# Gathered rows by each step's matmuls, a fixed order on ScalarE, and one later section of the top-k, in a hybrid S5 / mLSTM / PEER layer

## The chip, the cores and the metric

The kernel runs on one core of one Trainium2 chip. The metric is the device time of one execution in microseconds, from the first to the last instruction and what lies around them; lower is better. A core has TensorE (matrix products, "PE" in the profile, with "PEld" for its weight loads), VectorE ("DVE"), ScalarE ("ACT"), GpSimd ("POOL") and SyncE ("SP"), which here only starts transfers. Each engine works through its own queue in order, and waits on semaphores for the others.

## The reference

One decoder layer over 512 tokens of 1024 numbers, with 16 learned tokens ahead of them. A state-space branch and a matrix-memory branch are merged and added to the input; behind them comes a PEER layer, which holds 16384 experts of one neuron each. The change touches PEER alone:

```python
def block(xb):
    q = (xb @ w_q).astype(f32).reshape(PEER_TOKEN_BLOCK, PEER_HEADS, 2, PEER_HALF)
    s = jnp.einsum('thid,hikd->thik', q, keys32)
    sv, si = lax.top_k(s, PEER_TOPK)
    cand = sv[..., 0, :, None] + sv[..., 1, None, :]
...
    cs, ci = lax.top_k(cand, PEER_TOPK)
    eidx = jnp.take_along_axis(cidx, ci, axis=-1)
    gate = jax.nn.softmax(cs, axis=-1)
    ug = u_tab[eidx]
    act = jax.nn.gelu(jnp.einsum('td,thkd->thk', xb, ug).astype(f32))
    vg = v_tab[eidx]
    return jnp.einsum('thk,thkd->td', (gate * act).astype(vg.dtype), vg)
```

Each token has 8 heads; a head scores two sets of 128 keys and takes the best 16 of each, the best 16 of their sums name the experts (128 x 128 of them), and the token's output is the sum of the experts' rows of v, each weighted with its gate times the gelu of the token's product with the expert's row of u. The layer ends with a norm.

## The kernel before

The tokens are four tiles of 128. The kernel computes PEER in two ways side by side.

For 384 tokens (three tiles' worth, `SD`) it takes all experts as a dense product. The experts are 128 key columns of 128 experts each. For a column `j`, `hidden` (L1090) makes the products h of the column's block of u with 352 of those tokens (24 matmuls of 352 columns: eight blocks of the inner dimension, times three, since each operand is split into a high and a low part, and low times low is left out) and their gelu, `acts[j]`. The last 32 of the 384 are served through gathered rows in an earlier stage, whose values are copied. The gates of all 384 tokens, which are zero for most experts, come from DRAM tiles `gds` and `gd`. `w = gate * act` is then the weight matrix of the column, and `products` (L1593) adds w times the column's block of v to three PSUM accumulators (18 matmuls of 512 columns).

For one tile of 128 tokens it gathers rows instead: 128 rows per token from u and 128 from v, one row for all 128 tokens at a time (512 KB) by an indirect DMA on GpSimd (`fetch`, L1136). `use` (L1142) takes each: a product with the token and a sum for a row of u, a multiply-add into `ac0` for one of v. The first eight of these 256 are used ahead of the loop (`NEARLY`), 248 in it.

The loop over the columns (L1638 to L1699) is the last stage. In step `j`:
- `ready(j + 6)`: for 76 columns (`SP_`) the activations were made earlier and saved, and are loaded again in pairs; eight columns (`LEFT`) are made just ahead of the loop; for the other 44, which come in pairs, `hidden(j + 6)` splits the block of u (`uh` on ScalarE, `ul` on VectorE), makes h on TensorE and applies the gelu on ScalarE.
- the gates of eight columns at a time, `gin`, are loaded; the block of v is loaded (`raw`).
- VectorE multiplies `w`, ScalarE copies 32 columns more into it and makes its high part `wh` (L1656); `split` (L81) makes `vh` on ScalarE and `vl` on VectorE.
- gathered rows: `upto` says how many have to be used by the end of the step, an equal number a step. One is used ahead of `wl` (L1671, VectorE), the rest behind it.
- `products`, three times (the last three steps are done together by accumulator).

`wh`, `wl`, `vh` and `vl` have three buffers each, the PSUM tile of h two, the gathered rows seven.

What orders the instructions: a scheduler takes them in the order in which they are traced, moves each to where it expects it to be ready first, and so fixes each engine's queue before the run. `tc.keep_in_program_order(ins)` pins an instruction behind the one traced last on the same engine; `inorder` (L1061) does that inside the loop alone. In the loop VectorE's instructions are pinned; ScalarE's `vh`, copy, `wh`, `uh` and gelu are not.

Ahead of the loop, `scores(s)` (L1207) runs for 16 segments (8 heads times 2): a query product, its scores and their top 16 on VectorE. GpSimd makes the low part of each segment's weights (`wql`, in `split` with GpSimd). At segment 8 the generator `pairs_of(1, 0, 4)` (L1232) is run out: the candidates, their top 16, and the places of the chosen experts for four heads of token tile 1. It yields nine times; its last section (from L1298) makes the expert's number `ef`, the softmax, the offset `off` in the DRAM tile of gates, and turns both by 24 small matmuls into `xp`, from which GpSimd later scatters the gates column by column (`scatter`, from segment 13 on). `filled` puts pieces of `hidden` (a quarter column each) between the sections as work for TensorE.

Of the kernel before, what the change touches and what calls it, by code (L numbers as in the profile page):

```python
# [17 lines left out]
AF = mybir.ActivationFunctionType  # L18
# [5 lines left out]
P = 128  # L24
# [18 lines left out]
PH = 8  # L43
NKEY = 128
TOPK = 16
NSEG = 2 * PH
# [3 lines left out]
TB = 32  # L50
MS = TB
JB = 8
# [9 lines left out]
def f32(ap):  # L62
    return ap.bitcast(F32)
# [3 lines left out]
def tile_hybrid_block(ctx: ExitStack, tc: tile.TileContext, a: dict, out: bass.AP, dbg: dict | None = None):  # L67
    nc = tc.nc
    V, A, PE, GP, SY = nc.vector, nc.scalar, nc.tensor, nc.gpsimd, nc.sync
# [8 lines left out]
    ident = cst.tile([P, P], F32, name="ident")  # L78
    make_identity(nc, ident)

    def split(hi, lo, src, eng=V):  # L81
        A.activation(hi, src, AF.Copy)  # L82
        return eng.tensor_tensor(lo, src, f32(hi), op=OP.subtract)  # L83

    def mm3(ps, lh, ll, rh, rl, first, last, pin=None):
# [940 lines left out]
def peer(tc, a, out, dbg, cst, dram, xh, xl, blanks, ident, h2d, xsd, gds, x0, qt01, dump, split, mm3, rsqrt_cols):  # L1026
# [3 lines left out]
    V, A, PE, GP, SY = nc.vector, nc.scalar, nc.tensor, nc.gpsimd, nc.sync  # L1030
    NTD = NT - 1
    SD = NTD * P
    SDH = SD - MS
    RA = 6
    LEFT = 8
# [3 lines left out]
    SP_ = [2 * k + n for k in SPP for n in range(2)]  # L1039
    NEARLY = 8  # L1040
# [11 lines left out]
    with es:  # L1052
# [4 lines left out]
        ad = dram.tile([NSP, P, 2, SDH], F32, name="ad")  # L1057
        acts = {}
        loop = [False]

        def inorder(ins):  # L1061

            if loop[0]:
                tc.keep_in_program_order(ins)
            return ins
# [5 lines left out]
        def act_of(j):  # L1071

            k, n = divmod(j, 2)
            if k not in pairs_:
                pairs_[k] = up.tile([P, 2, SDH], F32, tag="act", name=f"act{k}", bufs=5)
            return (pairs_.pop(k) if n else pairs_[k])[:, n]

        def load(j, eng):

            k, n = divmod(j, 2)  # L1080
            if k not in uraw:
                uraw[k] = up.tile([P, 2, NK, P], F32, tag="uraw", name=f"u{k}", bufs=2)
                SY.dma_start(uraw[k], a["ut"][k])
            raw = (uraw.pop(k) if n else uraw[k])[:, n]
            hi = up.tile([P, NK, P], F32R, tag="uhi", name=f"uh{j}", bufs=3)
            lo = up.tile([P, NK, P], F32R, tag="ulo", name=f"ul{j}", bufs=3)
            inorder(split(hi, lo, raw, eng))
            return hi, lo

        def hidden(j, k0=0, k1=NK, eng=V, pin=False):  # L1090

            if k0 == 0:
                acts[j] = *load(j, eng), hps.tile([P, D // 2], F32, tag="h", name=f"h{j}")[:, :SDH]
            hi, lo, p = acts[j]
            clock[0] += (k1 - k0) * 0.48
            for k in range(k0, k1):
                mm3(p, hi[:, k], lo[:, k], xh[k // 4][:, k % 4, P:P + SDH], xl[k // 4][:, k % 4, P:P + SDH],
                    k == 0, k == NK - 1, tc.keep_in_program_order if pin and k == 0 else None)
            if k1 == NK:
                whole_ = pairs_.get(j // 2)  # L1100
                acts[j] = act_of(j)
                A.activation(acts[j], p, AF.Gelu_apprx_tanh)  # L1102
                if j in SP_:
                    acts.pop(j)
                    if j % 2:
                        SY.dma_start(ad[SPP.index(j // 2)], whole_)
# [430 lines left out]
        def filled(*of):  # L1537
            for us in pairs_of(*of):
                fill(us)
                yield  # L1540

        for s_ in range(NSEG):
            scores(s_)
            if s_ == 1:
                for r in range(P // MS):
                    SY.dma_start(xrep[MS * r:MS * (r + 1)], xsd)
            if s_ == NSEG // 2:
                for _ in filled(1, 0, PH // 2):
                    pass
            if s_ > NSEG - 4:  # L1550
                scatter(2)
# [25 lines left out]
        for j, h in todo:  # L1577
            hidden(j, 2 * h, 2 * h + 2)
# [56 lines left out]

        due = 0
        loop[0] = True
        for j in range(NKEY):  # L1638
            if j + RA < NKEY:
                ready(j + RA)  # L1640
            if j % JB == 0:
                gin = vp.tile([P, SD // TB, JB, TB], F32, tag="gin", name=f"gi{j}")
                i_ = SY.dma_start(gin[:, :HB], gds[:, j // JB])
                for o in heads[-1]:
# [3 lines left out]
            w = vp.tile([P, SD], F32, tag="w", name=f"w{j}", bufs=3)  # L1648
            raw = up.tile([P, D], F32, tag="vraw", name=f"v{j}", bufs=4)
            SY.dma_start(raw, a["v"][j // 2 * 2 * P:(j // 2 + 1) * 2 * P].rearrange("(p n) d -> p n d", n=2)[:, j % 2])  # L1650
            inorder(V.tensor_tensor(w[:, :SDH].rearrange("p (b t) -> p b t", t=TB), gin[:, :SDH // TB, j % JB],  # L1651
                                    acts.pop(j).rearrange("p (b t) -> p b t", t=TB), op=OP.mult))
            A.copy(w[:, SDH:], gin[:, SDH // TB, j % JB])
            wh = vp.tile([P, SD], F32R, tag="wh", name=f"wh{j}", bufs=3)
            wl = vp.tile([P, SD], F32R, tag="wl", name=f"wl{j}", bufs=3)
            A.activation(wh, w, AF.Copy)  # L1656
            vh = vp.tile([P, D], F32R, tag="vhi", name=f"vh{j}", bufs=3)
            vl = vp.tile([P, D], F32R, tag="vlo", name=f"vl{j}", bufs=3)
            inorder(split(vh, vl, raw))

            upto = min(j + 1, NKEY - 6) * (2 * P - NEARLY) // (NKEY - 6)
            for last in (0, 1):
                while due < (upto if last else min(due + 1, upto)):
                    n = NEARLY + due
# [115 lines left out]
```

## Time and profile before

| | |
|---|---|
| time, median of 3 runs | 1668.21 us (1667.74 to 1668.38) |
| profiled execution, its own time | 1670.1 us |
| its span | 1668.4 us |
| TensorE busy | 1620.0 us, 97% |
| VectorE busy | 1318.1 us, 79% |
| ScalarE busy | 708.3 us, 42% |
| GpSimd busy | 709.4 us, 43% |
| moved by DMA | 423.20 MB, mean 254 GB/s |
| the loop on TensorE, first to last product | 950.2 to 1656.6 us |

In a row of the timeline stand the start, the duration, engine, line, operation, the tiles written and read, shapes and a count; in square brackets, how long the engine was idle ahead of it and what ended that. A matmul's duration is modelled and overlaps the next one's, so the distance from start to start says what one costs. In a row of groups the mean is in nanoseconds. In a row of waits stand the engine and line that waited, what for, the total in us, how often, and the longest.

### The profile page before, as it was taken

How to read it: one execution, taken by the hardware profiler on the slowest of the kernel's cores; microseconds unless marked ns; L12 is line 12 of the kernel's file. 1: busy time of each engine (PE TensorE's matmuls, PEld its weight loads, DVE VectorE, ACT ScalarE, POOL GpSimd, SP SyncE). 2: the span in 40 equal slices, each digit the busy share in tenths (PEclk: the TensorE clock that was granted, in tenths of full speed). 3: DMA queues.
4: the chain of work that ended last, by engine and by line, in shares of the span. 5: the costliest groups of instructions: out<-in, count | busy, mean ns of one | idle time of the engine just before them, and what ended most of it. 6: DMA issues, size and time to landing. Idle time of an engine off the chain costs nothing.

```text
span 1668.4 us, 25647 instructions
## 1 busy us (share of the span) xinstructions
PE 1620.0 (97%) x9551; PEld 1429.4 (86%) x9551; DVE 1318.1 (79%) x2639; ACT 708.3 (42%) x1159; POOL 709.4 (43%) x474
## 2 busy tenths in 40 slices
PE   7999999999999999989999999999999999999997
PEld 7898787777889799989999888888888888888885
DVE  6996743366578899998798497988878989797976
ACT  4444554423333144565475533433343433343434
POOL 2000023213122477768877243434434756464630
PEclk9999999999999999999999999999999999999999
DMA  4514253113463256878999999999999999999973
GB/s 180 128 52 114 78 186 106 64 51 103 150 218 102 68 137 171 275 265 279 311 366 348 364 396 373 342 401 342 384 343 403 397 386 370 386 374 354 397 269 113
DMA packets 147957, 423.20 MB, mean 254 GB/s; under 512 B 38228, under 2 KB 56788, under 8 KB 138360
## 3 DMA queue, kind: packets, MB, share of 16 engines
q1 hardware_dynamic: 86184, 263.00, 43.9%
q0 software_dynamic: 55360, 151.07, 25.5%
q10 hardware_dynamic: 6288, 7.49, 1.4%
q8 instruction: 75, 1.23, 0.3%
q14 instruction: 50, 0.41, 0.1%
HBM read 376.13 MB, written 45.38 MB: 253 GB/s over the span
## 4 chain that ended last, share of the span: by engine, by line
PE 80%; DVE 8%; DMA 5%; ACT 2%; issue 2%; POOL 2%; ACTq 0%; DVEq 0%; POOLq 0%
PE o L86 10%; PE o L90 10%; PE o L89 10%; PE h L86 8%; PE h L90 8%; PE h L89 8%; PE q L89 1%; PE gp L1501 1%; PE q L90 1%; PE q L86 1%; DMA wo<-in_w_out 1%; PE s L877 1%; PE n L886 1%; POOL ge L1362 1%; DMA ge<-in_u,xsi 1%
## 5 line engine op out<-in xcount | busy, mean ns | idle before, releaser
L90 PE MATMUL h<-x2h,ul 128*128 128x352 f32 x1024 | 332.5, 325 | 5.3 <-DVE ul L83 5.3
L86 PE MATMUL h<-x2h,uh 128*128 128x352 f32 x1024 | 333.7, 326 | 3.7 <-ACT act L1102 1.8
L89 PE MATMUL h<-x2l,uh 128*128 128x352 f32 x1024 | 331.7, 324 | 0.0
L86 PE MATMUL o<-vh,wh 128*128 128x512 f32 x768 | 279.6, 391 | 7.7 <-ACT wh L1656 7.5
L89 PE MATMUL o<-vl,wh 128*128 128x512 f32 x768 | 278.9, 390 | 0.8 <-DVE vl L83 0.8
L90 PE MATMUL o<-vh,wl 128*128 128x512 f32 x768 | 266.3, 390 | 0.9 <-DVE wl L1671 0.9
L1139 POOL DMA_INDIRECT g<-in_v,e x128 | 202.2, 1580 | 146.5 <-DVE ac L1154 129.5
L82 ACT ACTIVATE uh<-u 128x1024 fp32r<-128x1024 f32 x128 | 135.2, 1059 | 224.5 <-PE h L89 170.9
L1139 POOL DMA_INDIRECT g<-in_u,e x120 | 135.2, 1126 | 214.1 <-DVE g L1146 195.4
L1421 POOL DMA_INDIRECT gds<-cw,ix x96 | 183.1, 1908 | 43.9 <-issue 28.6
L86 PEld LDWEIGHTS h<-x2h,uh 128*128 128x128 f32 x1024 | 193.4, 189 | 8.1 <-ACT act L1102 2.5
L90 PEld LDWEIGHTS h<-x2h,ul 128*128 128x128 f32 x1024 | 193.0, 189 | 8.0 <-DVE ul L83 6.7
L89 PEld LDWEIGHTS h<-x2l,uh 128*128 128x128 f32 x1024 | 193.2, 189 | 1.9
L82 ACT ACTIVATE vh<-v 128x1024 fp32r<-128x1024 f32 x128 | 135.1, 1057 | 132.9 <-PE o L90 116.0
L83 DVE TENSOR_TENSOR ul<-u,uh 128x1024 fp32r<-128x1024 f32 x128 | 155.4, 1217 | 26.6 <-ACT uh L82 26.5
L86 PEld LDWEIGHTS o<-vh,wh 128*128 128x128 f32 x768 | 143.4, 188 | 37.0 <-ACT wh L1656 9.9
L83 DVE TENSOR_TENSOR vl<-v,vh 128x1024 fp32r<-128x1024 f32 x128 | 155.8, 1217 | 22.7 <-ACT vh L82 22.6
L90 PEld LDWEIGHTS o<-vh,wl 128*128 128x128 f32 x768 | 144.1, 188 | 31.9 <-DVE wl L1671 1.6
L89 PEld LDWEIGHTS o<-vl,wh 128*128 128x128 f32 x768 | 144.2, 188 | 30.6 <-DVE vl L83 1.4
L1154 DVE SCALAR_TENSOR_TENSOR ac<-g,w,ac 128x1024 f32<-128x1024 f32 x127 | 162.2, 1277 | 0.1
L1146 DVE SCALAR_TENSOR_TENSOR g<-g,x 128x1024 f32<-128x1024 f32 x120 | 145.9, 1217 | 0.0
L1656 ACT ACTIVATE wh<-w 128x384 fp32r<-128x384 f32 x128 | 66.8, 522 | 143.5 <-DVE w L1651 141.5
(553 smaller groups left out, 3037.6 us busy)
## 6 DMA issues: line engine op xcount, KB each, us to landing
u<-in_ut SPq DMA_DIRECT2D x64, 1024.0 KB
v<-in_v SPq DMA_DIRECT2D x128, 512.0 KB
gd<-stg SPq DMA_DIRECT2D x9, 2048.0 KB
gi<-gd SPq DMA_DIRECT2D x16, 1152.0 KB
ad<-act SPq DMA_DIRECT2D x38, 352.0 KB
act<-ad SPq DMA_DIRECT2D x38, 352.0 KB
wq<-in_w_q SPq DMA_DIRECT2D x14, 512.0 KB
gds<-qt SPq DMA_DIRECT2D x6, 1024.0 KB
```

Of the source, the lines that this page charges most:

```text
L82: A.activation(hi, src, AF.Copy)
L83: return eng.tensor_tensor(lo, src, f32(hi), op=OP.subtract)
L86: i_ = PE.matmul(ps, lh, rh, start=first, stop=False)
L89: PE.matmul(ps, lh, rl, start=False, stop=False)
L90: return PE.matmul(ps, ll, rh, start=False, stop=last)
L877: PE.matmul(p[:, :w], xk[kk][:, c0:c0 + P], qt[:, kk, T - w:], start=kk == 0, stop=kk == 1)
L886: PE.matmul(p, pm[:, OFF[j] + (i - j) * P:OFF[j] + (i - j + 1) * P], vt[:, j], start=j == 0, stop=False)
L1139: return GP.indirect_dma_start(out=t, out_offset=None, in_=a["u"] if s_ < P else a["v"], in_offset=bass.IndirectOffsetOnAxis(ap=e0[:, c:c ...
L1146: i_ = V.scalar_tensor_tensor(g, g, 1.0, x0, op0=OP.mult, op1=OP.mult, accum_out=hsl[:, c:c + 1])
L1154: i_ = V.scalar_tensor_tensor(ac0, g, w0[:, c:c + 1], ac0, op0=OP.mult, op1=OP.add)
L1421: i_ = GP.indirect_dma_start(out=gds.rearrange("i g b j t -> (i g b j t)").unsqueeze(1), out_offset=bass.IndirectOffsetOnAxis(ap=ix[:, c:c ...
L1656: A.activation(wh, w, AF.Copy)
```

## The change

- The rows gathered in the loop are dealt out in proportion to the matmuls of each step. `steps` gives 18 x 0.227 for the products, and 24 x 0.161 more for a step in which h of a column is made; `upto` follows the running sum up to step 122.
- On ScalarE, `vh` of a step is pinned, then the 32-column copy, then `wh`, each behind the one before. The gelu of a column is no longer issued right behind its products h: the column is kept in `behind_v`, and the gelu follows `wh` of the next step, pinned. `uh` is as before. What VectorE does in a step keeps its order.
- Of the generator at segment 8 eight sections are run there, and the last one after the scores of segment 9.

```diff
-    def split(hi, lo, src, eng=V):
-        A.activation(hi, src, AF.Copy)
+    def split(hi, lo, src, eng=V, pin=lambda i_: i_):
+        pin(A.activation(hi, src, AF.Copy))
         return eng.tensor_tensor(lo, src, f32(hi), op=OP.subtract)
...
+        behind_v = []
...
             if k1 == NK:
+                if loop[0]:
+                    behind_v.append((j, p))
+                    return
                 whole_ = pairs_.get(j // 2)
                 acts[j] = act_of(j)
                 A.activation(acts[j], p, AF.Gelu_apprx_tanh)
...
             if s_ == NSEG // 2:
-                for _ in filled(1, 0, PH // 2):
+                first = filled(1, 0, PH // 2)
+                for _ in range(2 + PH // 2 + 2):
+                    next(first)
+            if s_ == NSEG // 2 + 1:
+                for _ in first:
                     pass
...
+        steps = [18 * 0.227 + (24 * 0.161 if LEFT <= j + RA < NKEY and j + RA not in SP_ else 0) for j in range(NKEY)]
         for j in range(NKEY):
...
-            A.copy(w[:, SDH:], gin[:, SDH // TB, j % JB])
             wh = vp.tile([P, SD], F32R, tag="wh", name=f"wh{j}", bufs=3)
             wl = vp.tile([P, SD], F32R, tag="wl", name=f"wl{j}", bufs=3)
-            A.activation(wh, w, AF.Copy)
             vh = vp.tile([P, D], F32R, tag="vhi", name=f"vh{j}", bufs=3)
             vl = vp.tile([P, D], F32R, tag="vlo", name=f"vl{j}", bufs=3)
-            inorder(split(vh, vl, raw))
-
-            upto = min(j + 1, NKEY - 6) * (2 * P - NEARLY) // (NKEY - 6)
+            inorder(split(vh, vl, raw, pin=tc.keep_in_program_order))
+            tc.keep_in_program_order(A.copy(w[:, SDH:], gin[:, SDH // TB, j % JB]))
+            tc.keep_in_program_order(A.activation(wh, w, AF.Copy))
+            while behind_v and behind_v[0][0] < j + RA:
+                n, p = behind_v.pop(0)
+                acts[n] = act_of(n)
+                tc.keep_in_program_order(A.activation(acts[n], p, AF.Gelu_apprx_tanh))
+
+            upto = min(int((2 * P - NEARLY) * sum(steps[:j + 1]) / sum(steps[:NKEY - 6]) + 1e-6), 2 * P - NEARLY)
             for last in (0, 1):
                 while due < (upto if last else min(due + 1, upto)):
```

## The prediction

> **What bounds the kernel now.** I read the page first (engine shares, the chain), then the waits of TensorE, then the loop's own rows.
>
> ```profile
> span 1668.4 us, 25647 instructions
> ...
> PE 1620.0 (97%) x9551; PEld 1429.4 (86%) x9551; DVE 1318.1 (79%) x2639; ACT 708.3 (42%) x1159; POOL 709.4 (43%) x474
> ...
> PE 80%; DVE 8%; DMA 5%; ACT 2%; issue 2%; POOL 2%; ACTq 0%; DVEq 0%; POOLq 0%
> ```
>
> TensorE is the bound: 97% busy and 80% of the chain. No part of the change takes a matmul away, so all it can win is TensorE's waiting. The next rows are TensorE's waits from 940 us to the end (the loop over the 128 key columns and what follows): engine and line that waited, what for, us in all, times, the longest. Behind them stands one window of that loop: engines' busy time, then granted clock, DMA's busy share and GB/s.
>
> ```profile
> PE o L86 <- ACT wh L1656: 7.5, 6, 1.7
> PE o L90 <- DVE wl L1671: 0.9, 1, 0.9
> PE o L89 <- DVE vl L83: 0.8, 1, 0.8
> PE h L86 <- ACT act L1102: 0.6, 1, 0.6
> ```
>
> ```profile
> 1300.00:1400.00 100.00, 100.00 (x489) 87.03 (x488) 90.12 (x100) 38.57 (x68) 62.65 (x38) 1.00 1.00 381
> ```
>
> In this window TensorE never stops (100.00 of 100 us). The loop has 9.8 us of visible waits in all, 7.5 of them for `wh`, the high part of w that ScalarE makes. What stands ahead of one such `wh` in ScalarE's queue (steps counted from the loop's first `vh` and `wh`):
>
> ```profile
> 1030.17 1.05 ACT L82 ACTIVATE vh<-v 128x1024 fp32r<-128x1024 f32 x1
> 1031.12 0.51 ACT L1656 ACTIVATE wh<-w 128x384 fp32r<-128x384 f32 x1
> 1033.16 1.06 ACT L82 ACTIVATE vh<-v 128x1024 fp32r<-128x1024 f32 x1 [1.53 <-PE o L90]
> ...
> 1041.15 1.06 ACT L82 ACTIVATE vh<-v 128x1024 fp32r<-128x1024 f32 x1 [3.67 <-PE o L90]
> 1042.12 0.20 ACT L1653 COPY w<-gi 128x32 f32<-128x32 f32 x1
> 1042.22 0.52 ACT L1656 ACTIVATE wh<-w 128x384 fp32r<-128x384 f32 x1
> ```
>
> ```profile
> 1033.28 0.52 DVE L1651 TENSOR_TENSOR w<-gi,act 128x352 f32<-128x352 f32 x1
> 1042.77 0.56 DVE L1671 TENSOR_TENSOR wl<-w,wh 128x384 fp32r<-128x384 f32 x1 [6.69 <-ACT wh L1656]
> ```
>
> ```profile
> 1040.91 0.32 PE L86 MATMUL h<-x2h,uh 128*128 128x352 f32 x1
> 1041.06 0.32 PE L89 MATMUL h<-x2l,uh 128*128 128x352 f32 x1
> 1042.80 0.73 PE L86 MATMUL o<-vh,wh 128*128 128x512 f32 x2 [1.41 <-ACT wh L1656]
> ...
> 1133.19 0.50 PE L86 MATMUL o<-vh,wh 128*128 128x512 f32 x1 [1.41 <-ACT wh L1656]
> 1223.48 0.50 PE L86 MATMUL o<-vh,wh 128*128 128x512 f32 x1 [1.36 <-ACT wh L1656]
> 1531.87 0.50 PE L86 MATMUL o<-vh,wh 128*128 128x512 f32 x1 [1.41 <-ACT wh L1656]
> 1621.93 0.50 PE L86 MATMUL o<-vh,wh 128*128 128x512 f32 x1 [1.73 <-ACT wh L1656]
> ```
>
> The three `vh` are those of steps 16, 17 and 18, the two `wh` those of 15 and 16. w of step 16 was ready at 1033.80 (1033.28 + 0.52), but its `wh` stands behind `vh` of step 18, which waits until the products of step 15 give its buffer back. So TensorE ends step 15, does two matmuls of h, and waits while ScalarE does `vh` 18, a copy and then `wh` 16. The cost of one is more than its idle time, since a matmul's end is modelled and overlaps the next: 1042.80 - 1041.06 is 1.74 us, where two such matmuls start 0.15 apart (1041.06 - 1040.91), so about 1.58 lost. The other three of 1.4 are alike; the last, idle 0.32 more, is 1.9. The five cost 4 x 1.58 + 1.9 = 8.2 us.
>
> **High part of v, then of w, then the last activation.** No instruction is added to the loop. `vh`, the 32-column copy, `wh` and the activation are pinned in this order on ScalarE, and the activation of a column whose products h were made in step j comes in step j + 1. For step 16 that is `vh` 16, copy, `wh` 16, and only then `vh` 17 and 18: `wh` 16 comes right behind w (1033.80) and is 6 us early for TensorE. The pin has a gap: in a step that also splits a u block (44 of 128), `vh` is pinned behind `uh`, which itself floats, so `vh` may stand ahead of an older `wh` there. Steps 16, 32, 48, 104 and 120, where the five waits lie, split none. I take all five as gone: -8.2 us (bounds 0 and -8.2). New waits: `wh` j now queues behind `vh` j, which waits for v's DMA and for the products of step j - 3; behind it are copy, `wh`, the activation, then VectorE's `wl`, then the products of j. But `wh` waits for the products of j - 3 anyway (three buffers each), and TensorE still has two steps to do. The later activation feeds w five steps on; two PSUM buffers hold h, and columns come in pairs with at least two steps between pairs. Both 0.
>
> **The loop's first step** pays for the pin, for the last instruction on ScalarE ahead of `vh` 0 is now the activation of column 7.
>
> ```profile
> 937.73 2.95 ACT L82 ACTIVATE vh<-v 128x1024 fp32r<-128x1024 f32 x3 [2.15 <-DMA gd<-stg]
> ...
> 951.01 0.80 ACT L1102 ACTIVATE act<-h 128x352 f32<-128x352 f32 x2
> ```
>
> ```profile
> 949.01 0.53 DVE L1651 TENSOR_TENSOR w<-gi,act 128x352 f32<-128x352 f32 x1 [6.13 <-DMA gi<-gd]
> 949.46 1.22 DVE L83 TENSOR_TENSOR vl<-v,vh 128x1024 fp32r<-128x1024 f32 x1
> 950.59 1.22 DVE L1146 SCALAR_TENSOR_TENSOR g<-g,x 128x1024 f32<-128x1024 f32 x1
> ...
> 951.74 0.56 DVE L1671 TENSOR_TENSOR wl<-w,wh 128x384 fp32r<-128x384 f32 x1
> ```
>
> ```profile
> 942.03 0.43 PE L86 MATMUL h<-x2h,uh 128*128 128x352 f32 x1 [0.56 <-ACT act L1102]
> ...
> 949.71 0.32 PE L90 MATMUL h<-x2h,ul 128*128 128x352 f32 x1
> ...
> 952.35 0.50 PE L90 MATMUL o<-vh,wl 128*128 128x512 f32 x1 [0.88 <-DVE wl L1671]
> ```
>
> Before, three `vh` were done by 940.7. Now `vh` 0 follows an activation that can start at 950.07, when h ends (949.71 + 0.32 = 950.03): + 0.35 (0.80 - 0.45 for one of the pair) = 950.42, + 1.06 = 951.5 for `vl`, + 1.13 (950.59 - 949.46), + 1.15 (951.74 - 950.59) = 953.8 for `wl`, + 0.61 (952.35 - 951.74) = 954.4 for the matmul that went at 952.35: +2.1. Against it: the three `vh` no longer hold up the activation for which TensorE was idle 0.56 at 942.03, and lighter first steps, below, save perhaps 0.2. Together +1.3. Bounds: -0.3, if the chain starts that much sooner than I think, and +3.1, if a `uh`, as long as a `vh`, comes between.
>
> **Rows dealt out by products.** The loop uses 248 gathered rows, before about two a step; now in proportion to 18 x 0.227, plus 24 x 0.161 in the 44 steps with h: 1.52 rows in a light step, 2.95 in a heavy one (248 / 668.5 x 4.09 or x 7.95).
>
> VectorE's light step, from the rows of the first step: w 0.45 (949.46 - 949.01) + `vl` 1.13 + `wl` 0.56 + two rows at 1.15 = 4.4 against TensorE's 4.09; a heavy one has a `ul`, as long as a `vl`, more: 5.6 against 7.95. Four light and two heavy make 28.9 of VectorE against 32.3 of TensorE; after, 4 x 3.9 + 2 x 6.65 = 28.9 again. VectorE stays behind in light steps and catches up in heavy ones, and three buffers cover that: TensorE waited for it twice in the loop, 0.9 and 0.8, at the two ends. So 0. The price if cover fails: a heavy pair holds two more rows, so w of the next step is up to 2.3 us later; VectorE's 6.69 idle at 1042.77 covers it. Each row takes its gather on POOL and 512 KB with it, so transfers thin out in light steps, where `v` and the saved activations also come. Bounds -1.7 (0.9 + 0.8) and +2.3.
>
> **Places set out later.** The last section for four heads of token tile 1 (seven small VectorE operations, 24 small matmuls, two or three quarter columns of h, no DMA) is traced after segment 9's scores instead of ahead of them; its scatters start at segment 13 either way.
>
> ```profile
> 553.93 0.20 DVE L1315 TENSOR_SCALAR oi<-oi 128x64 int32<-128x64 int32 x1
> 554.16 2.31 DVE L1316 CAST off<-oi 128x64 f32<-128x64 int32 x1
> ```
>
> ```profile
> 554.06 2.36 POOL L83 TENSOR_TENSOR wql<-wq,wqh 128x1024 fp32r<-128x1024 f32 x1 [3.20 <-ACT wqh L82]
> ```
>
> ```profile
> 554.59 0.39 PE L90 MATMUL q<-x2h,wql 128*128 128x512 f32 x1
> 554.82 0.40 PE L86 MATMUL q<-x2h,wqh 128*128 128x512 f32 x1
> 557.08 0.24 PE L1321 MATMUL xp<-off,ident 128*64 128x32 f32 x1 [1.86 <-DVE off L1318]
> ```
>
> TensorE loses 557.08 - 554.82 - 0.23 = 2.0 us, because a cast of 64 columns, for which the instruction ahead of it took 0.20 us, took 2.31, and ended as POOL's split of a weight block did. Later in both queues the places have scores and queries ahead of them, so TensorE has work meanwhile: -2.0, bounds 0 and -2.0. The Trainium skill, "SBUF — State Buffer", section "Who interferes with whom", says that VectorE and GpSimd take a shared pair of ports as a lock, each for a whole instruction. The trace agrees with these two rows (2.31 beside 2.36). By it the gain hangs on where the next POOL split falls: if the cast meets another, the sum is 2.0 higher.
>
> **The sum** goes by the profiled execution, span 1668.4 (its own time is 1670.1; the runs' median is 1668.21, which I start from): 1668.2 - 8.2 - 2.0 + 1.3 = 1659.3. A change of 0.2%, 3.3 us, is about what a measurement of this kernel can tell from none.
>
> **The rivals.**
>
> Slower: the hold moves instead of going. ScalarE's `uh` waits long for TensorE, and everything of the step is now pinned behind it.
>
> ```profile
> ACT uh L82 <- PE h L89: 89.6, 18, 7.9
> ```
>
> If that reaches TensorE in the pairs with h, each pays about 1.58. With 22 pairs in the loop the 8.9 won are gone at six; at twelve it is 1659.3 + 12 x 1.58 = 1678. For it: 18 waits, up to 7.9 us. Against: those 18 stand in the loop now, and TensorE shows nothing of them; it waits for `wh` six times, five of them behind a `vh`. 0.09.
>
> Transfers set the loop.
>
> ```profile
> DMA packets 83069, 256.00 MB, mean 358 GB/s; under 512 B 7436, under 2 KB 25670, under 8 KB 80332
> ```
>
> This is 945 to 1660 us. If 358 GB/s were all there is, the loop would keep its length whatever ScalarE's order, and only the places would gain: 1668.2 - 2.0 = 1666. Against it, the window of 1300 carried 381 GB/s with TensorE at 100%. "HBM Reference", first table, of the Trainium skill gives 358 GB/s as a core's share, but adds that a core streaming alone gets above it; the 381 agrees with the addition. 0.06.
>
> Half of it: the gap in the pin leaves two or three of the waits, or the places meet POOL again: 1662 to 1665. 0.16.
>
> It doesn't do what it says: the scheduler had nearly this order, and other instructions float into the gaps: 1668. 0.04.
>
> **How the numbers follow.** The forecast, 1656 to 1662, has 0.65. Faster by over 0.2% (under 1664.9): that and most of "half of it", 0.79. Within 0.2%: transfers, no effect, the rest of the half, 0.12. Slower: 0.09. The low end takes the remaining loop waits (1.7) and the kind start (1.6 less): 1656; I set 1655.5. The high end leaves out slower and no effect: 1667.
>
> **What would show it.** Right: TensorE's row of waits for `wh` down to the loop's first step; `wh` of step 16 directly after its `vh`; the wait for `off` gone; the first `vh` after 950 or so, and a wait of 3 to 4 us there. Wrong: waits for `wh`, `vl` or act that recur once for every pair of h; POOL or DMA between TensorE's steps; a long wait at the places again.

## The result and the profile after

The changed kernel takes 1655.7 us (median of 6 runs, 1653.8 to 1658.9); the kernel before, in turn with it, 1668.3 (1667.7 to 1669.2). The ratio is 0.9924, 95% interval 0.9912 to 0.9937: 12.6 us faster, where 8.9 were forecast. The profiled execution took 1656.8 us, 13.3 less than that of before. 1655.7 lies in the stated range (1655.5 to 1667) by 0.2 us, and 0.3 us below the 1656 to 1662 that had most of the chance; the same kernel on another chip, told below, took 1654.8. So that the total came out in the range is in part luck: the largest term was right, others were too small or too dear.

The page of the changed kernel: span, then engines (busy us, share, instructions).

```profile
span 1655.1 us, 25605 instructions
...
PE 1619.0 (98%) x9551; PEld 1427.8 (86%) x9551; DVE 1319.5 (80%) x2639; ACT 709.8 (43%) x1159; POOL 696.4 (42%) x474
```

TensorE is as busy as before (1619.0 us against 1620.0) in a span 13.3 us shorter: what went is waiting. Its waits for `wh` from 940 us to the end (us in all, times, the longest):

```profile
PE o L86 <- ACT wh L1668: 3.1, 3, 1.6
```

The 7.5 us for `wh` are 3.1. Of the three that remain, one is the loop's start (1.0), one its end, and the longest is step 16 again, but for another cause. ScalarE, VectorE and TensorE around it (start, us, engine, line, operation, tiles, and in brackets the idle time before it with what ended it):

```profile
1022.82 1.05 ACT L82 ACTIVATE vh<-v 128x1024 fp32r<-128x1024 f32 x1
1023.78 0.20 ACT L1667 COPY w<-gi 128x32 f32<-128x32 f32 x1
1029.29 1.06 ACT L82 ACTIVATE uh<-u 128x1024 fp32r<-128x1024 f32 x1 [5.31 <-DMA u<-in_ut]
1034.35 0.52 ACT L1668 ACTIVATE wh<-w 128x384 fp32r<-128x384 f32 x1 [4.01 <-DVE w L1660]
1034.78 0.45 ACT L1672 ACTIVATE act<-h 128x352 f32<-128x352 f32 x1
1035.13 1.05 ACT L82 ACTIVATE vh<-v 128x1024 fp32r<-128x1024 f32 x1
```

```profile
1033.74 0.52 DVE L1660 TENSOR_TENSOR w<-gi,act 128x352 f32<-128x352 f32 x1 [7.38 <-DMA gi<-gds]
```

```profile
1034.93 0.98 PE L86 MATMUL o<-vh,wh 128*128 128x512 f32 x3 [1.58 <-ACT wh L1668]
```

The order is the one that was written: `vh` 16, copy, `wh` 16, activation, `vh` 17, with one floating `uh` in between. ScalarE no longer holds `wh` back; it waits for w, and VectorE's w waited 7.38 us for the gates of steps 16 to 23 to land. In the run of the same kernel told below this wait didn't reach TensorE.

Where the 13.3 us went is read by cutting the span at four matmuls. These are the rows of before at the cuts (the first of the score matmuls after 475 us, the last of them, the last gates matmul, the first and the last product of the loop; the score row of five starts its last 0.28 before its end):

```profile
476.03 0.38 PE L1223 MATMUL sc<-keys,qt 128*128 128x128 f32 x1 [0.46 <-ACT qt L987]
...
595.94 0.72 PE L1223 MATMUL sc<-keys,qt 128*128 128x128 f32 x5
...
926.54 0.22 PE L1501 MATMUL gp<-o,o 128*128 128x128 bf16 x1
...
950.21 0.50 PE L86 MATMUL o<-vh,wh 128*128 128x512 f32 x1 [0.18 <-ACT wh L1656]
...
1656.57 0.39 PE L90 MATMUL o<-vh,wl 128*128 128x512 f32 x1
```

And those of the changed kernel:

```profile
476.44 0.38 PE L1227 MATMUL sc<-keys,qt 128*128 128x128 f32 x1 [0.46 <-ACT qt L987]
...
593.33 0.72 PE L1227 MATMUL sc<-keys,qt 128*128 128x128 f32 x5
...
917.22 0.22 PE L1505 MATMUL gp<-o,o 128*128 128x128 bf16 x1
...
943.65 0.50 PE L86 MATMUL o<-vh,wh 128*128 128x512 f32 x1 [1.02 <-ACT wh L1668]
...
1643.38 0.39 PE L90 MATMUL o<-vh,wl 128*128 128x512 f32 x1
```

Scores (first to last) -3.0, gates stage (last score to last gates matmul) -6.7, from there to the loop +2.8, loop -6.6 (706.7 to 700.1), and 0.4 later at the first cut. The two gains ahead of the loop come with the clock. Windows of before (engines' busy time, then granted clock, DMA share, GB/s), and the same of the changed kernel:

```profile
555.00:563.00 8.00, 6.14 (x44) 4.91 (x44) 7.90 (x44) 0.00 (x0) 1.42 (x1) 0.79 0.22 66
735.00:745.00 10.00, 7.19 (x61) 6.04 (x59) 10.00 (x16) 9.96 (x13) 8.78 (x5) 0.92 1.04 353
745.00:755.00 10.00, 7.74 (x46) 7.61 (x47) 10.00 (x15) 2.34 (x4) 8.78 (x5) 0.73 0.43 111
```

```profile
555.00:563.00 8.00, 7.29 (x56) 5.77 (x55) 7.93 (x43) 1.21 (x3) 2.38 (x1) 1.00 0.24 66
735.00:745.00 10.00, 9.13 (x74) 8.20 (x73) 10.00 (x18) 9.10 (x11) 8.47 (x6) 1.00 0.61 181
745.00:755.00 10.00, 10.00 (x65) 10.00 (x64) 10.00 (x18) 1.90 (x4) 8.47 (x6) 1.00 1.03 355
```

In before, TensorE drops to the lower of its two levels (1.2 of 2.4 GHz) for a part of these windows, right after it has waited: for the places at 557, and for the rows below at 742 to 747. The mean clock of 0.79 over 8 us, and of 0.92 and 0.73 over 20, stands for some 1.7 and 3.5 us at full speed (an estimate from these rows: 0.21 x 8, and 0.08 x 10 + 0.27 x 10) on top of the waits. In the changed kernel both falls are gone. The forecast left the clock ahead of the loop out. TensorE's waits of before from 735 to 755 us:

```profile
PE h L90 <- DVE ul L83: 3.1, 1, 3.1
PE h L86 <- ACT uh L82: 1.4, 1, 1.4
PE h L86 <- ACT act L1102: 0.5, 1, 0.5
```

### The profile page after: what moved, and what is told of

Same layout as the page of the kernel before. It is cut to its first block, busy times and chain, and to the rows that moved or that the text cites. A ratio compares the mean times of both kernels' runs of the same rounds, so it can differ in the third digit from the quotient of the medians.

```text
span 1655.1 us, 25605 instructions
## 1 busy us (share of the span) xinstructions
PE 1619.0 (98%) x9551; PEld 1427.8 (86%) x9551; DVE 1319.5 (80%) x2639; ACT 709.8 (43%) x1159; POOL 696.4 (42%) x474
## 3 DMA queue, kind: packets, MB, share of 16 engines
q0 software_dynamic: 55360, 151.07, 25.8%
## 4 chain that ended last, share of the span: by engine, by line
PE 84%; DVE 9%; DMA 4%; issue 1%; ACT 1%; ACTq 0%; SPq 0%; DVEq 0%
PE o L90 9%; PE o L89 9%; PE o L86 9%; PE h L90 9%; PE h L86 8%; PE h L89 8%; DMA v<-in_v 2%; PE gp L1505 2%; PE q L89 1%; PE q L86 1%; PE q L90 1%; DVE ul L83 1%; PE s L877 1%; PE n L886 1%; DVE g L1150 1%
## 5 line engine op out<-in xcount | busy, mean ns | idle before, releaser
L90 PE MATMUL o<-vh,wl 128*128 128x512 f32 x768 | 270.5, 391 | 0.9 <-DVE wl L1684 0.8
L1143 POOL DMA_INDIRECT g<-in_v,e x128 | 191.2, 1494 | 155.7 <-DVE ac L1158 131.2
L1143 POOL DMA_INDIRECT g<-in_u,e x120 | 140.9, 1174 | 214.6 <-DVE g L1150 185.5
L82 ACT ACTIVATE uh<-u 128x1024 fp32r<-128x1024 f32 x128 | 134.7, 1060 | 210.2 <-PE h L89 189.2
L1425 POOL DMA_INDIRECT gds<-cw,ix x96 | 192.9, 2009 | 52.2 <-issue 25.9
L82 ACT ACTIVATE vh<-v 128x1024 fp32r<-128x1024 f32 x128 | 135.0, 1055 | 105.0 <-PE o L90 69.7
```

What stands on the lines that cost most here:

```text
L82: pin(A.activation(hi, src, AF.Copy))
L90: return PE.matmul(ps, ll, rh, start=False, stop=last)
L1143: return GP.indirect_dma_start(out=t, out_offset=None, in_=a["u"] if s_ < P else a["v"], in_offset=bass.IndirectOffsetOnAxis(ap=e0[:, c:c ...
L1425: i_ = GP.indirect_dma_start(out=gds.rearrange("i g b j t -> (i g b j t)").unsqueeze(1), out_offset=bass.IndirectOffsetOnAxis(ap=ix[:, c:c ...
```

## The experiments

All were timed in turn with the kernel before; "ratio" is to it as it ran beside them, with the 95% interval. Its median lay between 1668.0 and 1669.6 us from chip to chip (1669.6 beside places two segments later, the low part on VectorE, and v and w pinned), so kernels of different sets are compared by the ratio. The stretches are those of the profile, cut as above: scores, gates stage, to the loop, loop.

| kernel | median us (range, runs) | ratio | scores | gates | to loop | loop |
|---|---|---|---|---|---|---|
| before | 1668.3 (1667.7 to 1669.2, 6) | | 120.4 | 330.2 | 23.7 | 706.7 |
| changed | 1655.7 (1653.8 to 1658.9, 6) | 0.9924 [0.9912, 0.9937] | 117.3 | 323.4 | 26.4 | 700.1 |
| places alone | 1665.3 (1662.3 to 1668.6, 11) | 0.9982 [0.9974, 0.9991] | 117.4 | 324.2 | 25.8 | 708.3 |
| order alone | 1660.1 (1658.0 to 1664.8, 6) | 0.9953 [0.9941, 0.9965] | 120.4 | 329.0 | 24.7 | 698.0 |
| rows alone | 1668.1 (1664.5 to 1669.1, 11) | 0.9995 [0.9986, 1.0004] | 120.4 | 328.8 | 24.1 | 705.8 |
| order and rows | 1659.7 (1658.7 to 1661.6, 5) | 0.9948 [0.9935, 0.9961] | 118.8 | 329.4 | 24.8 | 698.8 |
| places two segments later | 1666.1 (1664.0 to 1672.0, 11) | 0.9987 [0.9977, 0.9997] | 117.8 | 324.2 | 25.0 | 708.2 |
| low part on VectorE | 1667.1 (1664.5 to 1670.3, 12) | 0.9987 [0.9979, 0.9996] | 116.9 | 329.2 | 26.7 | 705.3 |
| v and w pinned, activation not moved | 1906.5 (1896.3 to 1907.9, 5) | 1.1405 [1.1383, 1.1427] | 120.4 | 329.2 | 24.8 | 943.2 |
| changed, first steps free | 1655.4 (1654.6 to 1657.0, 5) | 0.9926 [0.9913, 0.9939] | 117.3 | 324.7 | 29.0 | 697.1 |
| changed, gates sooner | 1661.8 (1657.7 to 1664.9, 5) | 0.9958 [0.9945, 0.9971] | 117.4 | 323.6 | 26.6 | 708.7 |
| changed, both of these | 1659.1 (1653.9 to 1662.9, 6) | 0.9945 [0.9927, 0.9963] | 117.4 | 324.1 | 24.8 | 702.8 |
| changed, again | 1654.8 (1653.8 to 1659.4, 6) | 0.9930 [0.9917, 0.9942] | 117.4 | 325.1 | 26.9 | 696.8 |
| order, rows, low part on VectorE | 1658.9 (1658.1 to 1660.4, 5) | 0.9945 [0.9931, 0.9958] | 116.9 | 329.6 | 24.7 | 697.2 |

The changed kernel's two profiles differ by 0.1 in the scores, 1.7 in the gates stage and 3.3 in the loop: differences below that in one profile say nothing. Nor is a profiled execution its kernel's median: it took 1670.1 us with the kernel before, 1664.1 with places alone (median 1665.3) and 1664.9, the slowest of five, with the gates sooner.

### The three parts by themselves

**Places alone**, the kernel before with this hunk:

```
-                for _ in filled(1, 0, PH // 2):
+                first = filled(1, 0, PH // 2)
+                for _ in range(2 + PH // 2 + 2):
+                    next(first)
+            if s_ == NSEG // 2 + 1:
+                for _ in first:
...
```

> The kernel before with the later places alone. Theory A (the places start all that is won ahead of the loop): TensorE's wait at the places shrinks from 1.9 to under 1 us, the granted clock does not fall behind it (before: half for 3.4 us from 559 us), and the stage behind it, whose order shifts, no longer has its 5 us of waits near 742 us and the half clock for 6.8 us there; products of the loop start 8 to 9 us earlier, and the five waits for wh stay: 8 to 9 us faster. Theory B (the stage from 690 to 930 us gains from the order on ScalarE, whose vh no longer float ahead of the loop): the places give 2.0 of wait and 1.7 of clock, 3.7 us faster, and the waits near 742 stay.

**Order alone**: the pins of `vh`, copy and `wh`, and the activation set behind them; the rows as before.

```
-            A.copy(w[:, SDH:], gin[:, SDH // TB, j % JB])
-            A.activation(wh, w, AF.Copy)
-            inorder(split(vh, vl, raw))
+            inorder(split(vh, vl, raw, pin=tc.keep_in_program_order))
+            tc.keep_in_program_order(A.copy(w[:, SDH:], gin[:, SDH // TB, j % JB]))
+            tc.keep_in_program_order(A.activation(wh, w, AF.Copy))
+            while behind_v and behind_v[0][0] < j + RA:
...
```

> The kernel before with ScalarE's order in the loop alone. Theory A: nothing ahead of the loop moves; the loop's start costs 2 us, four of the five waits of 1.6 to 1.9 us for wh go and one stays: 4 to 5 us faster. Theory B: the stage from 690 to 930 us gains 5 us as well: 9 to 10 us faster.

**Rows alone**:

```
-            upto = min(j + 1, NKEY - 6) * (2 * P - NEARLY) // (NKEY - 6)
+            upto = min(int((2 * P - NEARLY) * sum(steps[:j + 1]) / sum(steps[:NKEY - 6]) + 1e-6), 2 * P - NEARLY)
```

> The kernel before with the rows dealt out by products alone. Theory A, as predicted: no effect by itself, since VectorE's time for four light and two heavy steps is 28.9 us either way: within 1 us of before, the five waits for wh at the same steps. Rival: the even pace of gathers and of VectorE is what takes waits out of the loop: three or more of the five go, 4 to 6 us faster.

**Order and rows**: the changed kernel without the places' hunk.

> The changed kernel without the later places: order and rows. Theory A: as the order alone, 4 to 5 us faster, with TensorE's wait at the places and both falls of its clock as before. If the rows help the order (fewer waits for w), 1 to 2 us more than the order alone; if they hurt it (w of the first step behind a heavy pair later), less.

Order gives 8.3 us by the medians (1660.1 against 1668.4 on its chip), places 3.1, rows nothing that can be told from 0, as the forecast had it. TensorE's waits for `wh` from 940 us on, with order alone and with rows alone:

```profile
PE o L86 <- ACT wh L1663: 1.5, 2, 1.0
```

```profile
PE o L86 <- ACT wh L1657: 7.1, 5, 1.7
```

Both theories of that set fail in their numbers. The first had everything outside the places as the loop's 4 to 5 us: order alone gives nearly twice that. The second had ScalarE's order speed up the gates stage: with order alone that stretch is 329.0, as with rows alone (328.8), and 324.2 only where the places are later. So each part acts in its own stretch: the order in the loop (706.7 to 698.0, the forecast's 8.2 for five waits), the places in the scores and in the gates stage.

With places alone the profile has the loop's first product 7.5 us earlier (942.72 against 950.21) and no wait at 742, nearly what the first theory asked, but the median is only 3.1 us lower. Some of that is the loop, 1.6 us longer there, which is within what two profiles of one kernel differ by; and the gain isn't there in every execution, as the granted clock of the single runs shows below.

### What the later places do

**The low part on VectorE.** The kernel before, with the low part of one weight block, which ran on GpSimd across the places' cast, on VectorE. The queues of TensorE, ScalarE and SyncE stay word for word.

```
-                lows.append(split(hi, lo, raw, GP))
+                lows.append(split(hi, lo, raw, V if s_ == 12 else GP))
```

> The kernel before with the low part of segment 12's query weight, the one that ran on GpSimd across the places' casts, on VectorE; the queues of TensorE, ScalarE and SyncE are word for word those of before, and VectorE's differs by that one instruction and the few beside it. Theory: two engines writing at once stretched the cast to 2.0 us; alone it takes 0.2 to 0.3. The idle time before the places' transposes falls from 1.9 to under 0.7, the granted clock stays whole at 559, and the kernel is 2 to 3.5 us faster (1.9 - 0.5 of wait, 1.7 of the lower clock), 1665 to 1666.5, with the stretch at 742 as before. Rival: the low part costs VectorE what the cast gives back (1.2 us at the same place), the wait stays at 1.5 or more and the time within 0.7 us of before, 1667.6 to 1669.

VectorE there, then the window of 555 us:

```profile
554.92 0.20 DVE L1316 CAST off<-oi 128x64 f32<-128x64 int32 x1
...
555.58 1.22 DVE L83 TENSOR_TENSOR wql<-wq,wqh 128x1024 fp32r<-128x1024 f32 x1
```

```profile
555.00:563.00 8.00, 8.00 (x60) 6.41 (x59) 7.90 (x46) 0.78 (x2) 0.00 (x0) 1.00 0.23 68
```

The cast that took 2.31 us beside GpSimd's split takes 0.20 without it, TensorE has no wait (8.00 of 8.00) and the clock stays whole: scores 116.9 against 120.4, -3.5, as the theory said. So the clash of the two engines caused this wait. The Trainium skill, "SBUF — State Buffer", section "Who interferes with whom", says that GpSimd and certain VectorE instructions (a cast can be one, one with two inputs in SBUF is another if GpSimd reads SBUF) block each other for a whole instruction at the ports they share. This pair agrees (2.31 and 0.20). The gates stage keeps its waits (3.4, 1.4, 0.5) and, but for 1.0 us, its length, 329.2: they don't come from the wait at the places.

By the medians the kernel is 2.5 us faster than before on its chip (1667.1 against 1669.6), as the theory had it in the difference, though not in its 1665 to 1666.5. Its profile loses 3.0 us of the 3.5 again on the way to the loop (26.7 against 23.7): TensorE waits 2.6 us there for an activation that stands behind the three early `vh`, and the clock falls once more, to a mean of 0.66 from 940 to 945 us.

The wait and the fall of the clock don't always come together. In the profile of order and rows the places cost the same wait of 1.9 us, but the clock stays whole; the window of 555 us there:

```profile
555.00:563.00 8.00, 6.14 (x52) 4.82 (x51) 7.90 (x40) 0.00 (x0) 1.97 (x1) 1.00 0.21 66
```

Its scores take 118.8, 1.6 less than the 120.4 of before: VectorE's and TensorE's queues there are those of before, so this is what the fall alone costs, near the 1.7 estimated above. The expectation of "both falls" for that kernel held for the second alone.

**Places two segments later**, otherwise as "places alone":

```
-            if s_ == NSEG // 2 + 1:
+            if s_ == NSEG // 2 + 2:
```

> The kernel before with the last section of the places two score segments later, not one; all else as before. Theory: what the places' shift gives comes from the wait of 1.9 us and the half clock at 559 us, which any distance ends, and not from the order of VectorE's queue near 742 us. Then this kernel reads 1665 to 1666.5, like the shift by one, whether or not the stretch at 742 keeps its waits of 3 us for ul and its 6.8 us at the lower clock. Rival: the shift by one won by the chance of a new order at 742. Then a kernel whose profile keeps the lower clock at 742 to 747 reads 1667.5 or more, and one whose profile has lost it reads 1665.

1666.1, as the shift by one within the intervals; the wait for `off` is 1.1 here, 0.7 there and in the changed kernel, and the clock is whole in all three. The stretch at 742 us loses its waits here too. So each of the two shifts ended both, and this kernel's profile can't tell which of them the gain comes from: the rival would have needed a profile that kept the fall at 742. The mean granted clocks of its eleven runs say more. Seven have 0.995 to 0.997 and take 1664.0 to 1666.5 us; four have 0.994, as the kernel before has (0.992 to 0.995), and take 1668.2 to 1672.0. With places alone the two runs at 0.994 are among the slower (1666.3 and 1668.6, the others 1662.3 to 1667.2). So a part of the gain comes and goes with the clock, and is lost in some executions; where the clock fell in those, no profile shows. All six runs of the changed kernel beside before have 0.996.

In the changed kernel the places met GpSimd once more, as "half of it" had it:

```profile
555.83 2.00 DVE L1322 SCALAR_TENSOR_TENSOR off<-ef,off 128x64 f32<-128x64 f32 x1
```

```profile
555.37 2.38 POOL L83 TENSOR_TENSOR wql<-wq,wqh 128x1024 fp32r<-128x1024 f32 x1 [6.78 <-ACT wqh L82]
```

```profile
557.89 0.24 PE L1325 MATMUL xp<-off,ident 128*64 128x32 f32 x1 [0.71 <-DVE off L1322]
```

An instruction of 0.23 us took 2.00, but TensorE had more queries ahead of the places and idled 0.71 instead of 1.86. So the clash didn't go: work in TensorE's queue covers most of it. With places two segments later `off` itself took 0.21, but an instruction ahead of it in the same chain, which takes 0.69 otherwise, ran beside a split of GpSimd (551.80, 2.55), and TensorE still waited 1.1:

```profile
552.13 2.77 DVE L1049 TENSOR_TENSOR m<-ge,rkd 128x1024 f16<-128x1024 f16 x1
```

**Order, rows and the low part**: "order and rows" with that same line.

> The changed kernel without the later places, and with segment 12's low part of the query weight on VectorE: the loop's new order and the rows, and the wait of 1.9 us at the places and the fall of the clock behind it taken away in another way. The queues of TensorE, ScalarE and SyncE are those of the run with order and rows alone (1659.7). Theory: of the 4 us that the later places give on top of that run, some 2.5 belong to the places' stretch at 555 to 562 and the rest to the stretch at 742 to 752, which stays here: 1657 to 1658, with waits of 3 us and more and the lower clock near 743. Rival: the later places give everything at 555 to 562 and the 742 stretch is paid back before the loop: 1655.5 to 1656.5.

1658.9, ratio 0.9945 against 0.9948 without the line: the 2 us of the scores stretch (118.8 to 116.9) are in the profile, but not resolved by the medians, and the gates stage stays at 329.6. Expected were 1657 to 1658, and the rival's 1655.5 is further off. What separates this kernel from the changed one is therefore the gates stage: in the seven profiles with later places it is 323.4 to 325.1, in the seven without 328.8 to 330.2. The waits at 742 to 747 and the clock's fall behind them are there in before, and not in the changed kernel; in before VectorE's queue has four dot products and three gate operations, 1.2 us each, ahead of the `ul` that TensorE waits for, and in the changed one `ul` comes between them. The edit touches none of these instructions. It moves, in the text, a section of twelve small ones (the seven of the prediction leave out `ef` and the softmax), some 180 us ahead of them, and from there on the scheduler orders the queues of VectorE, ScalarE and TensorE otherwise. Where only the low part moves, VectorE's queue keeps its order behind 562 us, and the waits at 742 stay. That it came out better is shown; that another shift of the places would also do it is shown only for one and two segments.

### What ScalarE's order does

**v and w pinned, activation not moved**: of "order alone", the pins stay and the activation stands where it was.

```
-                if loop[0]:
-                    behind_v.append((j, p))
-                    return
...
-            while behind_v and behind_v[0][0] < j + RA:
-                n, p = behind_v.pop(0)
...
```

> The kernel before with the loop's high part of v, copy and high part of w pinned in this order, and the activation of a column left where it was, not behind them. Theory: what made wh late was that ScalarE had the next pair's high part of u, the activation and vh ahead of it; with wh pinned right behind vh the five waits go whatever becomes of the activation: under 2 us of ScalarE's waits for wh in the loop, 1659 to 1661. Rival: the activation, which waits for TensorE's last product of a column, has to stand behind wh as well; left alone it stands ahead of some vh or wh and the waits stay, four or five of them, with 1665 to 1668.

Neither came: 1906.5 us, 14% slower than before. TensorE's waits from 940 us on, then ScalarE at one pair:

```profile
PE o L86 <- ACT wh L1659: 81.2, 47, 5.9
PE h L86 <- ACT act L1102: 65.7, 43, 6.8
```

```profile
1004.88 1.06 ACT L82 ACTIVATE uh<-u 128x1024 fp32r<-128x1024 f32 x1 [8.64 <-PE h L89]
1005.85 0.45 ACT L1102 ACTIVATE act<-h 128x352 f32<-128x352 f32 x1
1006.19 1.05 ACT L82 ACTIVATE vh<-v 128x1024 fp32r<-128x1024 f32 x1
1007.14 0.20 ACT L1658 COPY w<-gi 128x32 f32<-128x32 f32 x1
1007.38 0.52 ACT L1659 ACTIVATE wh<-w 128x384 fp32r<-128x384 f32 x1
```

`uh` waits 8.64 us for TensorE's products of the older column, the activation follows, and only then `vh`, copy and `wh`; TensorE, done with the column, idles for `wh`. The two engines wait for each other in turn, 47 and 43 times with 44 columns made in the loop, and a lower clock (mean 0.952 over the run, 0.994 in before) adds to it: the two waits make 147 us, and 0.048 of 1906 us is 91 at full speed, an estimate, where before has 10. This is the mechanism of the forecast's slower rival, in which everything of the step is pinned behind a `uh` that waits for TensorE. It was priced at 1.58 us a pair, which is 35 for all 22 pairs; it cost 237 (1906.5 against 1669.6 on its chip), since each wait was longer and the clock fell. The later activation is the only difference to order alone, so it is what keeps this away. The other half, the activation set behind w with nothing pinned, wasn't run.

**First steps free**: in the changed kernel the first three `vh` aren't pinned.

```
-            inorder(split(vh, vl, raw, pin=tc.keep_in_program_order))
+            inorder(split(vh, vl, raw, pin=tc.keep_in_program_order if j >= 3 else lambda i_: i_))
```

> The changed kernel with the first three steps' high part of v left where it would go by itself, not pinned behind column 7's activation; from step 3 on as changed. Theory: the loop's first product waits for the first gates, which land at 942.3 us, and for the copy and wh behind them; the high part of v stands only 0.5 us in their way, and its low part and the first uses wait with it. The start gains 0.5 to 1.5 us, the rest stays: 1654.2 to 1655.2 where the changed kernel reads 1655.7. Rival: the pin costs the start its whole 2.0 us and more, as the step from the last score to the first product grew by 2.8 us: 1653 or less. A second rival: the early high parts fill the three buffers and hold up a later column, no gain.

1655.4 against 1654.8 for the changed kernel on the same chip: no gain, and the second rival is the nearest. The three early `vh` wait for the last gates' store and hold up what stands behind them; ScalarE, then TensorE:

```profile
932.82 2.95 ACT L82 ACTIVATE vh<-v 128x1024 fp32r<-128x1024 f32 x3 [5.29 <-DMA gd<-stg]
```

```profile
937.11 0.66 PE L86 MATMUL h<-x2h,uh 128*128 128x352 f32 x1 [3.19 <-ACT act L1106]
```

Behind this wait the clock falls as well, and the way to the loop grows to 29.0 us; the window of 935 us:

```profile
935.00:940.00 5.00, 2.89 (x10) 2.89 (x11) 1.23 (x1) 3.36 (x5) 0.00 (x0) 0.68 1.05 385
```

And the loop's start hangs on the first gates in any case. VectorE's first w in the changed kernel:

```profile
942.34 0.52 DVE L1660 TENSOR_TENSOR w<-gi,act 128x352 f32<-128x352 f32 x1 [10.17 <-DMA gi<-gd]
```

It starts 25.1 us after the last gates matmul; in before 22.5 (949.01 - 926.54). The first product comes 1.3 us behind it, in before 1.2. So the stretch to the loop grew by the gates' way out to memory and back, not by the pin: with places alone, where nothing is pinned, that first w starts 24.6 us after the last gates matmul.

**Gates sooner**: each group's gates are loaded four steps ahead of their first use.

```
-            if j % JB == 0:
+            for g0 in [0] * (j == 0) + [j + 4] * (j % JB == 4 and j + 4 < NKEY):
...
-                i_ = SY.dma_start(gin[:, :HB], gds[:, j // JB])
+                i_ = SY.dma_start(gin[:, :HB], gds[:, g0 // JB])
...
-                SY.dma_start(gin[:, HB:], gd[:, :, j:j + JB].rearrange("b i j t -> i b j t"))
+                SY.dma_start(gin[:, HB:], gd[:, :, g0:g0 + JB].rearrange("b i j t -> i b j t"))
```

> The changed kernel with each group's gates load set out four steps sooner, all arithmetic the same. Theory: the wait of 1.6 us that is left at step 16 comes from the load of that group's gates, which stands behind six loads of v in SyncE's queue and lands at 1033.7; set out sooner it is there, VectorE's waits for it in the loop (28.5 us in 8) fall under 5, TensorE's 1.58 us go: 1653.8 to 1654.4. Rival: the gates land late because the queues are full, and sooner issues only push loads of v or u back: the wait of the same size comes back for another load, 1655.4 to 1657.

The rival, and worse than it said, 1661.8 us: VectorE no longer waits for gates inside the loop, and the loop is 9 to 12 us longer than in the changed kernel's two profiles (by the medians the kernel loses 6.9; the profile is of its slowest run). ScalarE there:

```profile
1052.55 1.06 ACT L82 ACTIVATE vh<-v 128x1024 fp32r<-128x1024 f32 x1 [10.42 <-DMA v<-in_v]
1053.52 0.20 ACT L1669 COPY w<-gi 128x32 f32<-128x32 f32 x1
1053.75 0.52 ACT L1670 ACTIVATE wh<-w 128x384 fp32r<-128x384 f32 x1
```

A load of v now lands late, `vh` waits 10.42 us for it, and copy and `wh` stand pinned behind. TensorE waits 1.1 and 1.0 us there, and its clock falls to a mean of 0.66 from 1055 to 1060 us. ScalarE's waits for v from 944 to 1640 us, in this kernel and in the changed one (whose other profile has 22.1 in 7):

```profile
ACT vh L82 <- DMA v<-in_v: 71.7, 20, 10.4
```

```profile
ACT vh L82 <- DMA v<-in_v: 35.2, 10, 9.4
```

**Both**: the two edits together.

> Both of these edits in the changed kernel. Theory: they add up, 2 to 3 us below the changed kernel, 1652.7 to 1653.9. Rival: the start and the gates load are one and the same limit, so that the two together give what the larger gives alone.

1659.1, with a wide spread (1653.9 to 1662.9): they don't add up, the sooner gates cost as before and the free first steps give nothing sure.

**The changed kernel again**, on the chip of these three:

> The changed kernel itself on the chip of the three others, as their base: 1655.7 within 1 us, and the same profile with one wait for wh in the loop after its start.

1654.8. Its waits for `wh` from 940 us on:

```profile
PE o L86 <- ACT wh L1668: 1.8, 2, 1.4
```

Step 16 is not among them: both are the loop's start and end. So the last wait inside the loop comes and goes with the landing of one load, and its 1.6 us are no fixed part of the changed kernel.

## Why the prediction was right, and where not

- **The five waits for `wh`, -8.2.** Right in mechanism and size: the loop is 6.6 and 9.9 us shorter in the two profiles of the changed kernel, 8.7 with order alone, which gives 8.3 by the medians and leaves 1.5 us of waits for `wh`. Two of the reasons beside it were too easy. "Both 0" for the later activation is right, but it is no harmless companion: without it the pin costs 237 us. And VectorE's reserve, which I counted as cover, is what now meets the gates' load: 28.5 us of waits in the loop where there were 0.9.
- **The loop's first step, +1.3.** Too dear. I built it on the end of h at 950.03, but what sets the start is the landing of the first gates: from VectorE's first w to the first product of `wl` it is 3.3 us in before and 3.6 and 3.3 in the changed kernel. The pin costs 0 to 0.3 there, and 0.3 with order alone. With order and rows, in two kernels, and with the gates sooner it is 0.7, 1.4 and 1.2: there column 7's h ends after the gates have landed, so the chain of the forecast does set the start, at about its price. The sign I named, a wait of 3 to 4 us at the first steps, isn't there: TensorE waits 1.0 and 0.6.
- **Places, -2.0.** This step is mis-sized twice. The wait for `off` is not gone, it fell from 1.86 to 0.71, since the split on GpSimd was met again; the clock, which I had left out, is the other half of the 3.0 us of that stretch. And the forecast saw nothing in the gates stage, where the profile has another 6.7, of which the way of the gates to memory takes 2.8 back before the loop. By the medians the places are worth 3.1 alone and 4.0 on top of the other two parts, and single runs without that gain show the lower clock.
- **Rows, 0.** Right: 0.3 us, interval -2.3 to +0.7.
- **The rivals.** "Half of it" and "no effect" fell. "Transfers set the loop" fell as stated, since the order's gain came in full; but the run with gates sooner shows how little is left there. "Slower" did not come here; its mechanism is that of the kernel with the pin and the old activation.

The steps by the medians, each on top of the last: order 8.3, rows 0.4, places 4.0, some 12.6 in all. The forecast's 8.9 was short by a little over 1 at the loop's start and by 2 at the places. Measured each alone the three give 11.7, so that they add up is shown within the intervals; why the scheduler's order of VectorE's queue at 742 us is the better one with later places was not tried apart from them.

## What to carry to other kernels

Pin an engine's instructions as a chain or not at all: a pin lets each instruction wait for all that its forerunners wait for, so set the one that waits for the bound engine last, and look for what floats in between. Read the granted clock beside each wait of TensorE, in every stage and not only in the one that the change names: where the clock fell behind waits of 2 and 5 us here, they cost nearly as much again, though the same wait of 1.9 us once came without a fall, and the loop's five of 1.4 to 1.7 us left the clock whole. A profile shows one execution: set the mean clock of every run beside its time. An edit in the text moves the scheduler's queues far behind it, so a part's effect is taken from a run of that part alone, cut into stretches.

## What the runs showed of the hardware

The granted clock was lost in the middle of a busy stage: in before 1.9 us of idle time ahead of 557 us, and a mean of 0.79 from 555 to 563; in the changed kernel, idle 0.71 at the same place, 1.00; with order and rows, idle 1.9 and still 1.00. So the same wait came with a fall and without one, and what decides it these runs don't show. Two VectorE instructions on 64 columns took 2.31 and 2.00 us where they ran beside GpSimd's 2.4 us split, a cast in one kernel and an operation of two inputs in the other, and 0.20 to 0.23 where they did not. With DMA at 0.93 to 1.02 of its time from 950 to 1600 us, an earlier start of the gates' loads lengthened the loads of v from 10.2 to 12.3 us (medians from issue to landing; 9.7 in the changed kernel's other profile): a sooner load pushed a more urgent one back.
